# More pairs of k-tiles multiplied with seven block products in a three-product fp32r decoder trunk

## The chip, the cores and the metric

One core of one Trainium2 chip runs the whole program. The metric is the device time of one execution in microseconds (us).

## What is computed

Two decoder layers on 256 tokens of width 2048. Layer 0 mixes tokens by retention (8 heads, keys of 256, values of 512), layer 1 by multi-head latent attention; each mixer is followed by a SwiGLU with an inner width of 5632. The parts that the change touches are three products of the 256 tokens with a weight matrix:

```python
def retention(x, positions, w_in, gn_g, w_out):
    ...
    out = (jax.nn.silu(g.astype(jnp.float32)) * y).astype(x.dtype)
    return out @ w_out

def swiglu(x, w_gu, w_down):
    gate, up = jnp.split(x @ w_gu, [D_FF], axis=-1)
    return (jax.nn.silu(gate) * up) @ w_down
```

## The kernel before

**Splitting.** Every number of a matrix product is split into a high part (a cast to fp32r on ScalarE, here ACT, line 201) and a low part (value minus high part, on VectorE, here DVE, line 202), and a product is made of three matmuls on TensorE, here PE: high by high, high by low, low by high.

**Groups.** `group` multiplies two row tiles of 128 tokens (t = 0, 1) with 1024 columns of a weight matrix, over `kts` k-tiles of 128 rows, into four PSUM banks of 512 columns, b00, b01, b10 and b11 (row tile, column half). A weight tile is 128 x 1024: SyncE's queue (SP) loads it into one of 4 `raw` buffers, ACT writes its high part and DVE its low part, in 5 buffers each (`weights`, tags whi and wlo). An ordinary k-tile takes 12 matmuls of 128 x 512: 2 row tiles, 2 column halves, 3 products. Gate/up runs `group` 11 times per layer (slices j of 512 gate and 512 up columns, 16 k-tiles each), the down projection twice (halves of 1024 columns, 44 k-tiles), the retention output twice (32 k-tiles).

**Pairs by sevens.** Two k-tiles k0 and k1 form a 2 x 2 by 2 x 2 block product: the left side has four 128 x 128 blocks (row tile by k-tile), the right side four 128 x 512 blocks (k-tile by column half). For the pairs in `sevens`, `group` makes it with seven block products in place of eight, 21 matmuls in place of 24. The price is sums. Of the left blocks there are four (`left_sums`, lines 230 to 233, 128 x 128 each, then split into hi and lo, 512 wide); they are made once for gate/up and kept, and once per pair and half in `closing` (`parted`). Of the right blocks there are four too, made anew for each pair: t1 = b00 + b01 and t3 = b01 + b11 in the tile ta, t2 = t1 + b11 and t4 = t2 + b10 in tb (`right_sums`, lines 244 to 247, tsum, 2 buffers). ta and tb are split like weight tiles and take whi and wlo buffers; of tile k0 only the first half is split then, so that a pair by sevens holds four of the five buffers.

**Where the products go.** Products 2, 3 and 4 run straight into banks b00, b01 and b10. Products 1, 5, 6 and 7 have banks of their own (m1, m6 from the six `mm` banks, m5 and m7 the two `misc` banks), which gather over all pairs by sevens of a group. The last pair takes the products in the order 1, 6, 5, 7, 2, 3, 4, the others 1, 2, 3, 5, 7, 6, 4. Behind the last, `combine` (lines 334 to 337) copies m1 to SBUF and forms u and v, and `add` (lines 343 and 345) adds them to the four banks: those of row tile 0 one k-tile after the next (`after + 1`), those of row tile 1 two k-tiles later (`after + 3`).

**Gate/up's end.** After each slice ACT makes fsg (silu of the gate) and DVE fa (times up); fa is transposed on PE some k-tiles later (line 776) and copied by ACT to aT, the left side of the down projection.

**Order.** The program issues in the order of the plan that `group` writes, with small jobs put off by `later`. Each engine works its own queue in order; an instruction that waits holds up what is behind it. Names in the orders below: `gu0_3_w10` is k-tile 10 of slice 3 in layer 0; `_w5_ta` with its `tahi` and `talo` are the sums of pair 5; `mv0`, `mv1`, `mv2` are m1, u and v; `rto` is the retention output, `dn` the down projection.

Of the kernel before, what the change touches and what calls it, by code (L numbers as in the profile page):

```python
# [8 lines left out]
F32 = mybir.dt.float32  # L9
F32R = mybir.dt.float32r  # L10
# [5 lines left out]
P = 128  # L16
# [5 lines left out]
RH, RK, RV = 8, 256, 512  # L22
# [8 lines left out]
G_MIX, G_FFN, G_GN, G_Q, G_KV = 0, 32, 64, 96, 100  # L31
NG = 104

GU_SEVENS = (2, 4)
DN_SEVENS = (2, 6, 10, 14, 18)

C_INV, C_ID, C_MASK, C_TWICE = 0, NF, NF + P, NF + 3 * P
C_DEC = C_TWICE + ROPE
# [16 lines left out]
def trunk(  # L55
# [28 lines left out]
    def misc_bank(name):  # L84
        return ps.tile([P, 512], F32, tag="misc", bufs=2, name=name)
# [30 lines left out]
    def rsqrt(v, n, tag, bufs, name):  # L116
        r = small(n, tag, bufs, name)
        nc.gpsimd.tensor_tensor(out=r, in0=v, in1=mhalf[:, 0:n], op=ALU.pow)
        return r
# [9 lines left out]
    def later(k, fn):  # L129
        order[0] += 1  # L130
        todo.append((steps[0] + k, order[0], fn))
# [63 lines left out]
    wp = ctx.enter_context(tc.tile_pool(name="wp", bufs=1))  # L195
    RAW, WB = 4, 5

    def split(hi, lo, src, g=None):

        if g is None:  # L200
            nc.scalar.copy(out=hi, in_=src)  # L201
            nc.vector.tensor_sub(out=lo, in0=src, in1=hi.bitcast(F32))  # L202
        else:
            nc.scalar.activation(out=hi, in_=src, func=AF.Copy, scale=g)
            nc.vector.scalar_tensor_tensor(
                out=lo, in0=src, scalar=g, in1=hi.bitcast(F32), op0=ALU.mult, op1=ALU.subtract
            )
# [11 lines left out]
    def gain(col, kt):  # L219
        return None if col is None else gcol[:, col + kt : col + kt + 1]  # L220
# [370 lines left out]
    def retention():  # L591
# [32 lines left out]
        def vg_group(h):  # L624
            name = f"rvg{h}"
            return group(h_lhs, DT, tile_load(ret_vg, h, name), name)

        with tc.tile_pool(name="rt_s", bufs=1) as sp:
# [80 lines left out]
            with tc.tile_pool(name="rt_v", bufs=1) as rp:  # L709
                yT = rp.tile([P, RH * 4, NT, P], F32, name="yT")  # L710

                def mixed(h, t, pr, v, sg):
                    y = misc_bank(f"ry{h}{t}")

                    terms = [
                        (pr[a][:, (kb + t) * P : (kb + t + 1) * P], v[b][:, kb, :])
                        for kb in range(t + 1)
                        for a, b in ((0, 0), (0, 1), (1, 0))
                    ]
                    for n, (left, right) in enumerate(terms):  # L720
                        nc.tensor.matmul(y, left, right, start=n == 0, stop=n == len(terms) - 1)  # L721
                    st = rp.tile([P, 6], F32, tag="bst", bufs=4, name="bst")
                    nc.vector.bn_stats(out=st, in_=y)
                    mv = rp.tile([P, 2], F32, tag="bmv", bufs=4, name="bmv")
                    nc.vector.bn_aggr(out=mv, in_=st)
                    ve = rp.tile([P, 1], F32, tag="bve", bufs=4, name="bve")
                    nc.vector.tensor_scalar(ve, mv[:, 1:2], scalar1=EPS, scalar2=None, op0=ALU.add)
                    rs = rsqrt(ve, 1, "grs", 4, "grs")
                    z = rp.tile([P, RV], F32, tag="z", bufs=2, name="z")
                    nc.vector.scalar_tensor_tensor(  # L730
                        out=z, in0=y, scalar=mv[:, 0:1], in1=sg[:, t, :],
                        op0=ALU.subtract, op1=ALU.mult,
                    )
                    nc.vector.tensor_scalar(z, z, scalar1=rs, scalar2=None, op0=ALU.mult)

                    def transposes():
                        tp = misc_bank(f"ztp{h}{t}")
                        for j in range(4):
                            nc.tensor.transpose(
                                tp[:, j * P : (j + 1) * P], z[:, j * P : (j + 1) * P], ident  # L740
                            )
                        for j in range(4):
                            nc.scalar.activation(
                                out=yT[:, h * 4 + j, t, :], in_=tp[:, j * P : (j + 1) * P], func=AF.Copy,
                                scale=gain(G_GN, h * 4 + j),
                            )

                    later(4, transposes)

                for h in range(RH):  # L750
                    if h:
                        banks = vg_group(h)
                    vh = rp.tile([P, NT, RV], F32R, tag="vh", bufs=1, name=f"vh{h}")
                    vl = rp.tile([P, NT, RV], F32R, tag="vl", bufs=1, name=f"vl{h}")
                    ph = rp.tile([P, 3 * P], F32R, tag="ph", bufs=1, name=f"ph{h}")
                    pl = rp.tile([P, 3 * P], F32R, tag="pl", bufs=1, name=f"pl{h}")
                    split(ph, pl, scores[h])
                    sg = rp.tile([P, NT, RV], F32, tag="sg", bufs=1, name=f"sg{h}")
                    for t in range(NT):
                        split(vh[:, t, :], vl[:, t, :], banks[t][0], rx[t])  # L760
                        nc.scalar.activation(
                            out=sg[:, t, :], in_=banks[t][1], func=AF.Silu, scale=rx[t]
                        )
                    for t in range(NT):
                        later(2 + t, lambda h=h, t=t, pr=(ph, pl), v=(vh, vl), sg=sg: mixed(h, t, pr, v, sg))
                closing(lambda k0, n: yT[:, k0 : k0 + n], RH * 4, ret_out, g_mix_post[0], G_FFN, "rto")


    def swiglu(i):
        with tc.tile_pool(name=f"ff{i}", bufs=1) as fp:  # L770
            aT = fp.tile([P, FF // P, NT, P], F32, name=f"aT{i}")

            def transposes(j, t, a):
                tp = misc_bank(f"ftp{i}{j}{t}")
                for b in range(4):
                    nc.tensor.transpose(tp[:, b * P : (b + 1) * P], a[:, b * P : (b + 1) * P], ident)  # L776
                nc.scalar.copy(
                    out=aT[:, j * 4 : j * 4 + 4, t, :], in_=tp.rearrange("p (j q) -> p j q", j=4)
                )


            ins = {}
            held = {}

            def sums():
                return (
                    fp.tile([P, 4, P], F32, tag="sf", bufs=2, name=f"sf{i}"),
                    fp.tile([P, 4, P], F32R, tag="sa", bufs=4, name=f"sh{i}"),
                    fp.tile([P, 4, P], F32R, tag="sa", bufs=4, name=f"sl{i}"),
                )  # L790

            def seen(t, k0, n, part):
                for p in GU_SEVENS:
                    if k0 <= 2 * p < k0 + n:
                        held[t, p] = part[:, 2 * p - k0], part[:, 2 * p - k0 + 1]
                        if (1 - t, p) in held:
                            f, hi, lo = sums()
                            left_sums(*held[0, p], *held[1, p], f, hi, lo)
                            ins[p] = hi, lo

            watch[0] = seen

            for j in range(FF // 512):
                name = f"gu{i}_{j}"
                banks = group(
                    h_lhs, DT, tile_load(w_gu[i], j, name), name, lead=2 if j else 4,
                    sevens=GU_SEVENS if 0 < j else (), left=lambda p: ins[p],
                )
                watch[0] = None
                for t in range(NT):  # L810
                    sg = fp.tile([P, 512], F32, tag="fsg", bufs=2, name="fsg")
                    nc.scalar.activation(out=sg, in_=banks[t][0], func=AF.Silu, scale=rx_next[t])
                    a = fp.tile([P, 512], F32, tag="fa", bufs=2, name="fa")
                    nc.vector.scalar_tensor_tensor(
                        out=a, in0=banks[t][1], scalar=rx_next[t], in1=sg, op0=ALU.mult, op1=ALU.mult
                    )
                    later(2 + t, lambda j=j, t=t, a=a: transposes(j, t, a))
            closing(
                lambda k0, n: aT[:, k0 : k0 + n], FF // P, w_down[i], g_ffn_post[i],
                None if i else G_MIX + DT, f"dn{i}", sevens=DN_SEVENS, sums=sums,  # L820
            )

# [272 lines left out]


    retention()
    swiglu(0)
    mla()
# [92 lines left out]
```

## Time and profile before

| | |
|---|---|
| median of 3 runs | 2454.28 us (2453.28 to 2454.59) |
| the profiled execution | 2454.15 us |
| its span | 2452.3 us, mean granted clock 0.999 |
| PE matmul, weight load | 2438.9 us (99%), 2023.6 us (83%) |
| DVE, ACT | 1799.4 us (73%), 1311.1 us (53%) |

The span runs from the first to the last instruction of the profiled execution. A matmul row lasts longer than its distance to the next one, because matmuls are pipelined; so what one costs is read from stretches of many. PEld is the load of the stationary operand, which runs beside the matmuls.

### The profile page before, as it was taken

What the parts mean: (1) busy time and instruction counts of PE and PEld (TensorE: products, weight loads), DVE (VectorE), ACT (ScalarE), POOL (GpSimd) and SP (SyncE); (2) the same over time, 40 slices, a digit from 0 to 9 for tenths busy, and PEclk for the clock granted to TensorE, in tenths of its full rate; (3) what the DMA queues carried; (4) which work ended last, traced back from release to release, by engine and by line L of the source; (5) the groups of instructions that cost most, each with busy time, mean ns of one, the idle gap of its engine ahead of it and who ended that gap; (6) DMA issues with size and microseconds to landing.
All of it is one profiled execution on the core that took longest, in us unless ns stands there. A gap on an engine that the chain in (4) does not pass through costs nothing.

```text
span 2452.3 us, 30456 instructions
## 1 busy us (share of the span) xinstructions
PE 2438.9 (99%) x11128; PEld 2023.6 (83%) x11128; DVE 1799.4 (73%) x2379; ACT 1311.1 (53%) x1751; POOL 27.1 (1%) x38
## 2 busy tenths in 40 slices
PE   9999999999999999999999999999999999999998
PEld 7888888888888888888888888888888888888887
DVE  7655555555657787787888887876778777788887
ACT  5434544445545554555556666655555554556664
POOL 0000000000000000000000000000000000000000
PEclk9999999999999999999999999999999999999999
DMA  7555555555565566565656655445556656565664
GB/s 261 186 185 178 182 181 181 180 181 181 198 197 189 172 211 200 182 212 180 207 181 210 208 198 162 129 134 193 188 174 210 197 185 211 187 200 183 214 204 155
DMA packets 129607, 463.75 MB, mean 189 GB/s; under 512 B 14640, under 2 KB 15024, under 8 KB 129456
## 3 DMA queue, kind: packets, MB, share of 16 engines
q1 hardware_dynamic: 129456, 461.80, 57.1%
q8 instruction: 87, 1.43, 0.2%
q14 instruction: 64, 0.52, 0.1%
HBM read 459.64 MB, written 2.10 MB: 188 GB/s over the span
## 4 chain that ended last, share of the span: by engine, by line
PE 99%; DMA 0%; DVE 0%; SPq 0%; ACT 0%; issue 0%; DVEq 0%; POOL 0%; POOLq 0%; ACTq 0%
PE gu_b L398 34%; PE dn_b L398 17%; PE rvg_b L398 14%; PE rto_b L398 7%; PE rqk_b L398 7%; PE gu_m L398 4%; PE mlo_b L398 4%; PE q L398 3%; PE dn_m L398 2%; PE mc_b L398 2%; PE ftp L776 1%; PE ry L721 1%; PE htp L434 1%; PE asc L1032 0%; PE rsc L676 0%; PE asc L1029 0%
## 5 line engine op out<-in xcount | busy, mean ns | idle before, releaser
L398 PE MATMUL gu_b<-gu_w_hi,hT 128*128 128x512 f32 x2256 | 640.8, 392 | 0.0
L201 ACT CAST gu_w_hi<-gu_w_raw 128x1024 fp32r<-128x1024 f32 (+1 forms) x352 | 349.4, 1003 | 327.7 <-PE gu_b L398 252.3
L202 DVE TENSOR_TENSOR gu_w_lo<-gu_w_raw,gu_w_hi 128x1024 fp32r<-128x1024 f32 (+1 forms) x352 | 402.7, 1159 | 120.3 <-ACT gu_w_hi L201 120.0
L398 PEld LDWEIGHTS gu_b<-gu_w_hi,hT 128*128 128x128 f32 x2256 | 419.4, 188 | 85.7 <-DVE hT L202 0.9
L398 PE MATMUL gu_b<-gu_w_lo,hT 128*128 128x512 f32 x1128 | 358.2, 390 | 0.0
L398 PE MATMUL rvg_b<-rvg_w_hi,hT 128*128 128x512 f32 x1024 | 280.8, 391 | 0.0
L202 DVE TENSOR_TENSOR rvg_w_lo<-rvg_w_raw,rvg_w_hi 128x1024 fp32r<-128x1024 f32 x128 | 156.4, 1224 | 160.6 <-ACT rvg_w_hi L201 160.6
L398 PEld LDWEIGHTS gu_b<-gu_w_lo,hT 128*128 128x128 f32 x1128 | 211.5, 188 | 44.8 <-DVE gu_w_lo L202 0.6
L201 ACT CAST rvg_w_hi<-rvg_w_raw 128x1024 fp32r<-128x1024 f32 x128 | 134.7, 1053 | 195.8 <-PE rvg_b L398 187.4
L201 ACT CAST dn_w_hi<-dn_w_raw 128x1024 fp32r<-128x1024 f32 (+1 forms) x176 | 174.3, 1003 | 104.1 <-PE dn_b L398 55.9
L398 PEld LDWEIGHTS rvg_b<-rvg_w_hi,hT 128*128 128x128 f32 x1024 | 191.1, 188 | 38.9
L202 DVE TENSOR_TENSOR dn_w_lo<-dn_w_raw,dn_w_hi 128x1024 fp32r<-128x1024 f32 (+1 forms) x176 | 200.0, 1160 | 23.6 <-ACT dn_w_hi L201 22.9
L398 PE MATMUL dn_b<-dn_w_hi,dn_ah 128*128 128x512 f32 x564 | 178.2, 390 | 0.0
L398 PE MATMUL dn_b<-dn_w_lo,dn_ah 128*128 128x512 f32 x564 | 178.0, 390 | 0.0
L398 PE MATMUL dn_b<-dn_w_hi,dn_al 128*128 128x512 f32 x564 | 178.0, 390 | 0.0
L398 PE MATMUL rvg_b<-rvg_w_lo,hT 128*128 128x512 f32 x512 | 158.1, 390 | 0.0
L398 PE MATMUL rqk_b<-rqk_w_hi,hT 128*128 128x512 f32 x512 | 141.0, 393 | 2.0 <-ACT hT L201 1.0
L398 PEld LDWEIGHTS dn_b<-dn_w_lo,dn_ah 128*128 128x128 f32 x564 | 105.9, 188 | 22.0
L398 PEld LDWEIGHTS dn_b<-dn_w_hi,dn_al 128*128 128x128 f32 x564 | 105.9, 188 | 21.9
L398 PEld LDWEIGHTS dn_b<-dn_w_hi,dn_ah 128*128 128x128 f32 x564 | 105.6, 188 | 21.6
L202 DVE TENSOR_TENSOR rqk_w_lo<-rqk_w_raw,rqk_w_hi 128x1024 fp32r<-128x1024 f32 (+1 forms) x65 | 77.5, 1207 | 59.3 <-ACT rqk_w_hi L201 59.3
L201 ACT CAST rqk_w_hi<-rqk_w_raw 128x1024 fp32r<-128x1024 f32 (+1 forms) x65 | 67.4, 1038 | 99.4 <-PE rqk_b L398 90.2
(307 smaller groups left out, 3851.6 us busy)
## 6 DMA issues: line engine op xcount, KB each, us to landing
gu_w_raw<-w_gu SPq DMA_DIRECT2D x352, 512.0 KB, 4.3
dn_w_raw<-w_down SPq DMA_DIRECT2D x176, 512.0 KB, 4.4
rvg_w_raw<-ret_vg SPq DMA_DIRECT2D x128, 512.0 KB, 3.5
rto_w_raw<-ret_out SPq DMA_DIRECT2D x64, 512.0 KB, 3.5
rqk_w_raw<-ret_qk SPq DMA_DIRECT2D x63, 512.0 KB, 4.0
mlo_w_raw<-mla_out SPq DMA_DIRECT2D x32, 512.0 KB, 3.5
uq_w_raw<-mla_up SPq DMA_DIRECT2D x32, 448.0 KB, 3.4
mc_w_raw<-mla_c SPq DMA_DIRECT2D x16, 512.0 KB, 4.6
```

The costliest lines, as they stand in the source:

```text
L201: nc.scalar.copy(out=hi, in_=src)
L202: nc.vector.tensor_sub(out=lo, in0=src, in1=hi.bitcast(F32))
L398: nc.tensor.matmul(out, e[2](), e[3](), start=bank not in begun, stop=ends[bank, bank in added] == n, skip_group_check=bank in added,)
L434: nc.tensor.transpose(tp[:, j * P : (j + 1) * P], xs[:, t, (k0 + j) * P : (k0 + j + 1) * P], ident)
L721: nc.tensor.matmul(y, left, right, start=n == 0, stop=n == len(terms) - 1)
L776: nc.tensor.transpose(tp[:, b * P : (b + 1) * P], a[:, b * P : (b + 1) * P], ident)
```

## The change

The tables at the top of the file choose the pairs. Gate/up takes pairs 2, 3 and 5 of its eight (before: 2 and 4), from slice 1 on; the down projections every third pair, six of 22 (before: every fourth, five); the retention output takes three of 16, for the first time. The third left sums of gate/up live in the buffers of `closing`'s split activations (tags ah and al, 3 each); those of the retention output in buffers of the heads, which are done by then.

```diff
-GU_SEVENS = (2, 4)
-DN_SEVENS = (2, 6, 10, 14, 18)
+GU_SEVENS = (2, 3, 5)
+DN_SEVENS = (2, 5, 8, 11, 14, 17)
+RTO_SEVENS = (2, 6, 10)
...
-                closing(lambda k0, n: yT[:, k0 : k0 + n], RH * 4, ret_out, g_mix_post[0], G_FFN, "rto")
+
+                def sums():
+                    both = ("vh", "vl")[sums.n % 2]
+                    sums.n += 1
+                    s = rp.tile([P, 2, 4, P], F32R, tag=both, bufs=1, name="rs")
+                    f = rp.tile([P, 4, P], F32, tag="sg", bufs=1, name="rsf")
+                    return f, s[:, 0], s[:, 1]
+
+                sums.n = 0
+                closing(
+                    lambda k0, n: yT[:, k0 : k0 + n], RH * 4, ret_out, g_mix_post[0], G_FFN, "rto",
+                    sevens=RTO_SEVENS, sums=sums,
+                )
...
-            def sums():
-                return (
-                    fp.tile([P, 4, P], F32, tag="sf", bufs=2, name=f"sf{i}"),
-                    fp.tile([P, 4, P], F32R, tag="sa", bufs=4, name=f"sh{i}"),
-                    fp.tile([P, 4, P], F32R, tag="sa", bufs=4, name=f"sl{i}"),
-                )
+            def sums(n=0):
+                f = fp.tile([P, 4, P], F32, tag="sf", bufs=2, name=f"sf{i}")
+                if n < 2:
+                    hi = fp.tile([P, 4, P], F32R, tag="sa", bufs=4, name=f"sh{i}")
+                    lo = fp.tile([P, 4, P], F32R, tag="sa", bufs=4, name=f"sl{i}")
+                else:
+                    hi = wp.tile([P, 4, P], F32R, tag="ah", bufs=3, name=f"sh{i}")
+                    lo = wp.tile([P, 4, P], F32R, tag="al", bufs=3, name=f"sl{i}")
+                return f, hi, lo
...
-                            f, hi, lo = sums()
+                            f, hi, lo = sums(len(ins))
```

**DVE, the last pair by sevens of a gate/up slice** (slice 3 of layer 0). Before, from the first low part behind pair 4's sums to tile 10:

```order
L202 TENSOR_TENSOR gu0_3_w6_lo_7172<-gu0_3_w6_raw_7169,gu0_3_w6_hi_7171 128x1024
L202 TENSOR_TENSOR gu0_3_w7_lo_7190<-gu0_3_w7_raw_7187,gu0_3_w7_hi_7189 128x1024
L202 TENSOR_TENSOR gu0_3_w8_lo_7208<-gu0_3_w8_raw_7205,gu0_3_w8_hi_7207 128x512
L202 TENSOR_TENSOR gu0_3_w9_lo_7214<-gu0_3_w9_raw_7211,gu0_3_w9_hi_7213 128x1024
L202 TENSOR_TENSOR gu0_3_w4_talo_7224<-gu0_3_w4_ta_7217,gu0_3_w4_tahi_7223 128x1024
L202 TENSOR_TENSOR gu0_3_w4_tblo_7228<-gu0_3_w4_tb_7218,gu0_3_w4_tbhi_7227 128x1024
L202 TENSOR_TENSOR gu0_3_w10_lo_7262<-gu0_3_w10_raw_7259,gu0_3_w10_hi_7261 128x1024
```

After, from the low part of pair 3's second sum on:

```order
L203 TENSOR_TENSOR gu0_3_w3_tblo_7369<-gu0_3_w3_tb_7359,gu0_3_w3_tbhi_7368 128x1024
L245 TENSOR_TENSOR gu0_3_w5_ta_7441<-gu0_3_w10_raw_7429 128x512
L203 TENSOR_TENSOR gu0_3_w8_lo_7396<-gu0_3_w8_raw_7393,gu0_3_w8_hi_7395 128x1024
L203 TENSOR_TENSOR gu0_3_w9_lo_7414<-gu0_3_w9_raw_7411,gu0_3_w9_hi_7413 128x1024
L203 TENSOR_TENSOR gu0_3_w10_lo_7432<-gu0_3_w10_raw_7429,gu0_3_w10_hi_7431 128x512
L246 TENSOR_TENSOR gu0_3_w5_ta_7441<-gu0_3_w10_raw_7429,gu0_3_w11_raw_7435 128x512
L203 TENSOR_TENSOR gu0_3_w11_lo_7438<-gu0_3_w11_raw_7435,gu0_3_w11_hi_7437 128x1024
L247 TENSOR_TENSOR gu0_3_w5_tb_7442<-gu0_3_w5_ta_7441,gu0_3_w11_raw_7435 128x512
L203 TENSOR_TENSOR gu0_3_w5_talo_7448<-gu0_3_w5_ta_7441,gu0_3_w5_tahi_7447 128x1024
L248 TENSOR_TENSOR gu0_3_w5_tb_7442<-gu0_3_w5_tb_7442,gu0_3_w11_raw_7435 128x512
L203 TENSOR_TENSOR gu0_3_w5_tblo_7452<-gu0_3_w5_tb_7442,gu0_3_w5_tbhi_7451 128x1024
```

Before, the sums of the last pair (four of them, earlier than this piece) were made ahead of the low parts of the two ordinary tiles 6 and 7; now they stand between the low parts of tiles 8 to 11, behind the second sum of the pair two before.

**DVE, the end of the same slice**, from the additions of row tile 0 on. Before:

```order
L345 TENSOR_TENSOR gu0_3_b00_7030<-gu0_3_b00_7030,gu0_3_mv0_7252 128x512
L345 TENSOR_TENSOR gu0_3_b01_7031<-gu0_3_b01_7031,gu0_3_mv1_7253 128x512
L202 TENSOR_TENSOR gu0_3_w14_lo_7339<-gu0_3_w14_raw_7336,gu0_3_w14_hi_7338 128x1024
L345 TENSOR_TENSOR gu0_3_b10_7032<-gu0_3_b10_7032,gu0_3_mv2_7254 128x512
L202 TENSOR_TENSOR gu0_3_w15_lo_7357<-gu0_3_w15_raw_7354,gu0_3_w15_hi_7356 128x1024
L343 TENSOR_TENSOR gu0_3_mv2_7254<-gu0_3_m5_7146,gu0_3_mv2_7254 128x512
L202 TENSOR_TENSOR gu0_4_w0_lo_7387<-gu0_4_w0_raw_7384,gu0_4_w0_hi_7386 128x1024
L345 TENSOR_TENSOR gu0_3_b11_7033<-gu0_3_b11_7033,gu0_3_mv2_7254 128x512
```

After:

```order
L346 TENSOR_TENSOR gu0_3_b00_7207<-gu0_3_b00_7207,gu0_3_mv0_7476 128x512
L346 TENSOR_TENSOR gu0_3_b01_7208<-gu0_3_b01_7208,gu0_3_mv1_7477 128x512
L203 TENSOR_TENSOR gu0_4_w0_lo_7575<-gu0_4_w0_raw_7572,gu0_4_w0_hi_7574 128x1024
L346 TENSOR_TENSOR gu0_3_b10_7209<-gu0_3_b10_7209,gu0_3_mv2_7478 128x512
L203 TENSOR_TENSOR gu0_4_w1_lo_7587<-gu0_4_w1_raw_7584,gu0_4_w1_hi_7586 128x1024
L344 TENSOR_TENSOR gu0_3_mv2_7478<-gu0_3_m5_7323,gu0_3_mv2_7478 128x512
L203 TENSOR_TENSOR gu0_4_w2_lo_7617<-gu0_4_w2_raw_7614,gu0_4_w2_hi_7616 128x1024
L346 TENSOR_TENSOR gu0_3_b11_7210<-gu0_3_b11_7210,gu0_3_mv2_7478 128x512
```

The additions to b10 and b11 stood among the low parts of the slice's last tiles and the next slice's first; now they stand two tiles further on, behind tiles 0, 1 and 2 of the next slice. The additions belong to the slice's last k-tile.

**ACT, the start of the retention output.** Before:

```order
L201 CAST rto0_w4_hi_4646<-rto0_w4_raw_4644 128x1024
L201 CAST rto0_w5_hi_4664<-rto0_w5_raw_4662 128x1024
L201 CAST rto_ah_4640<-yT_2007 128x512
L201 CAST rto0_w6_hi_4686<-rto0_w6_raw_4684 128x1024
L201 CAST rto0_w7_hi_4713<-rto0_w7_raw_4711 128x1024
```

After:

```order
L202 CAST rto0_w4_hi_4654<-rto0_w4_raw_4652 128x512
L202 CAST rto0_w5_hi_4660<-rto0_w5_raw_4658 128x1024
L202 CAST rto_ah_4648<-yT_2007 128x512
L202 CAST rto0_w2_tahi_4670<-rto0_w2_ta_4664 128x1024
L202 CAST rto0_w2_tbhi_4674<-rto0_w2_tb_4665 128x1024
L202 CAST rto_ah_4703<-yT_2007 128x512
L202 CAST rto0_w6_hi_4709<-rto0_w6_raw_4707 128x1024
L202 CAST rto0_w7_hi_4736<-rto0_w7_raw_4734 128x1024
L202 CAST rs_4586<-rsf_4587 128x512
```

The two casts of the sums come in ahead of tile 6, and rs, the split left sums of pair 2 (tiles 4 and 5), stands behind the casts of tiles 6 and 7.

## Rows read from the trace of the kernel before

**Rows 1.** Totals of the page, and busy tenths in 40 slices of the span

```profile
PE 2438.9 (99%) x11128; PEld 2023.6 (83%) x11128; DVE 1799.4 (73%) x2379; ACT 1311.1 (53%) x1751; POOL 27.1 (1%) x38
...
PE   9999999999999999999999999999999999999998
...
DVE  7655555555657787787888887876778777788887
...
PEclk9999999999999999999999999999999999999999
```

**Rows 2.** PE's waits: line, releaser, us in total, times, longest

```profile
PE warm L95 <- DVE mhalf L111: 1.2, 1, 1.2
PE rqk_b L398 <- ACT hT L201: 1.0, 1, 1.0
PE rqk_b L398 <- ACT rqk_w_hi L201: 1.0, 1, 1.0
PE htp L434 <- DMA xs<-x: 0.8, 2, 0.6
PE rqk_b L398 <- DVE rqk_w_lo L202: 0.3, 1, 0.3
PE htp L434 <- DVE xs L497: 0.2, 1, 0.2
```

**Rows 3.** The chain of waits: start us, us, engine, tile, line, instructions

```profile
599.13 149.65 PE rto_b L398 x660
...
1039.57 23.80 PE gu_b L398 x105
...
1246.26 17.00 PE dn_b L398 x75
1267.34 17.00 PE dn_b L398 x75
```

**Rows 4.** The page's costliest groups: one matmul and one weight load of gate/up

```profile
L398 PE MATMUL gu_b<-gu_w_hi,hT 128*128 128x512 f32 x2256 | 640.8, 392 | 0.0
...
L398 PEld LDWEIGHTS gu_b<-gu_w_hi,hT 128*128 128x128 f32 x2256 | 419.4, 188 | 85.7 <-DVE hT L202 0.9
```

**Rows 5.** Timeline of DVE in a gate/up slice: start, us, instruction, idle time before it

```profile
1016.29 0.68 DVE L202 TENSOR_TENSOR gu_w_lo<-gu_w_raw,gu_w_hi 128x512 fp32r<-128x512 f32 x1
1016.89 0.69 DVE L246 TENSOR_TENSOR gu_w_tb<-gu_w_ta,gu_w_raw 128x512 f32<-128x512 f32 x1
1017.61 0.69 DVE L247 TENSOR_TENSOR gu_w_tb<-gu_w_tb,gu_w_raw 128x512 f32<-128x512 f32 x1
1020.02 1.23 DVE L202 TENSOR_TENSOR gu_w_lo<-gu_w_raw,gu_w_hi 128x1024 fp32r<-128x1024 f32 x1 [1.72 <-ACT gu_w_hi L201]
...
1024.78 0.69 DVE L245 TENSOR_TENSOR gu_w_ta<-gu_w_raw 128x512 f32<-128x512 f32 x1 [1.40 <-DMA gu_w_raw<-w_gu]
...
1047.47 1.22 DVE L202 TENSOR_TENSOR gu_w_lo<-gu_w_raw,gu_w_hi 128x1024 fp32r<-128x1024 f32 x1
1048.60 0.69 DVE L343 TENSOR_TENSOR gu_mv<-gu_m,gu_mv 128x512 f32<-128x512 f32 x1
```

**Rows 6.** ACT's groups by form: count, busy us, mean ns, idle before

```profile
L201 ACT CAST gu_w_tahi<-gu_w_ta 128x1024 fp32r<-128x1024 f32 x40 | 42.1, 1054 | 12.5 <-PE gu_b L398 12.2 <-DVE sf L233 0.3
...
L201 ACT CAST sh<-sf 128x512 fp32r<-128x512 f32 x24 | 14.8, 616 | 2.0 <-DVE sf L233 1.7
```

**Rows 7.** Timeline of DVE in the down projection of layer 0

```profile
1303.86 1.23 DVE L202 TENSOR_TENSOR dn_w_tblo<-dn_w_tb,dn_w_tbhi 128x1024 fp32r<-128x1024 f32 x1 [1.47 <-ACT dn_w_tbhi L201]
...
1306.61 4.63 DVE L202 TENSOR_TENSOR dn_w_lo<-dn_w_raw,dn_w_hi 128x1024 fp32r<-128x1024 f32 x4 [0.26 <-ACT dn_w_hi L201]
```

**Rows 8.** One gate/up slice: PE, PEld, DVE, ACT, POOL, clock, DMA share, GB/s

```profile
1003.81:1046.88 43.07, 43.07 (x195) 35.70 (x194) 33.78 (x39) 22.62 (x25) 0.00 (x0) 1.00 0.59 195
```

**Rows 9.** DMA issues of the page: count, size of one, median us to landing

```profile
gu_w_raw<-w_gu SPq DMA_DIRECT2D x352, 512.0 KB, 4.3
```

## Prediction

> **What bounds the kernel now.** I read the totals of the page first. PE is busy 2438.9 us of 2452.3 at full granted clock in every slice, while DVE is busy 73% of the span, ACT 53%; DVE stands at seven or eight tenths in nearly every slice from the 13th on, where gate/up and the down projections lie [rows 1]. A busy PE need not be a PE without waits, so the list of PE's waits comes next: its six rows add up to 4.5 us, all at the start or between layers [rows 2]. The chain of waits agrees: long stretches of matmuls, one after the other. Such a stretch gives the price of a matmul: 23.80 us for 105 in gate/up, 17.00 for 75 in the down projection, 149.65 for 660 in the retention output, 0.2267 us each time [rows 3]. A matmul's own row lasts 0.392 us [rows 4], because its end lies some 0.17 us behind the next one's start; that is no cost, but it is the delay with which a buffer comes free. So every matmul is on the path, and whatever takes matmuls away shortens the kernel, as long as operands come in time.
>
> **What the change takes away.** A pair of k-tiles costs 24 matmuls, a pair by sevens 21. Gate/up has 10 slices per layer with sevens (slice 0 has none): one pair more in each of 20 slices is 60 matmuls. A down projection has 2 halves and two layers, one pair more (six for five) in each of 4 halves: 12. The retention output gets three pairs in each of 2 halves: 18. Together 90, which is also what PE's order shows (10532 rows before, 10442 now, no new ones). 90 x 0.2267 = **20.4 us**: 13.6, 2.7 and 4.1. There are also 30 x 0.68 us fewer of cover for the other engines.
>
> A rule of the Trainium skill speaks for a smaller sum: "TensorE: Matmul & The Clock Gate", section "Back-to-back issue gap", gives about 131 ns per matmul for a stream of weight loads and matmuls of 512 columns; by it the 90 would be worth an estimated 11.8 us. The trace disagrees with 226.7 ns in each of the three stages that the change touches, and the sum goes by the trace.
>
> **What it adds.** For each of the 30 pairs, four sums of 512 columns on DVE (three of 0.60 us start to start and one of 0.72 where it waits for the one before, from 1016.29, 1016.89 and 1017.61), and the low parts of two 1024-wide tiles (1.13 each, as from 1047.47 to 1048.60) [rows 5]; the low part of the pair's first tile shrinks by half (-0.53). That is 3 x 0.60 + 0.72 + 2 x 1.13 - 0.53 = 4.25 us of DVE. ACT gets two casts of 1.05 and saves 0.44 on the halved one (1.05 to 0.62) [rows 6], 1.7 us. Left sums are made per pair in the retention output and the down projections, and once per layer for gate/up: four narrow adds, one 0.62 cast and one low part of 0.60 each [rows 6]. SP's queue keeps its 80 entries; one of them, a load of post-norm gains, stands one place earlier, and nothing waits for it before its half has ended: nothing. The rest costs only where PE waits for it, so I go through the three stages.
>
> *Down projections (4 halves).* Two ordinary pairs lie between sevens now, three before; the cycle of four pairs is 21.08 us (from 1246.26 to 1267.34 [rows 3]). DVE's queue stands idle 1.47 us before the second sum's low part, since the cast before it waits for a buffer that PE holds, and 0.26 us before the run of four low parts that follows [rows 7]. That buffer comes free about 2.7 us before the pair begins; cast (1.05) and low part (1.23) end 0.4 us before the pair's start, and PE asks for them 3.4 us into it, behind 15 matmuls. Slack 3.8 us: nothing lost, 2.7 us gained. DVE's work per three pairs is some 14.3 us of 15.6.
>
> *Retention output (2 halves).* Between sevens lie three ordinary pairs, as in the down projections before, which had no wait: 4.1 us. One exception is the start of half 0. On ACT the cast of pair 2's left sums (rs) stands behind the casts of tiles 6 and 7, and that of tile 7 needs the buffer of tile 4, which PE holds for the first three matmuls of pair 2 (0.68 + 0.17 us). So rs is ready at 0.85 + 1.05 + 0.62 and some handover, 2.6 to 2.9 us into the pair; PE wants it after six matmuls, at 1.36. **About 1.5 us lost, once.** Below, 0, if tile 7's cast does not wait; above 2.5, with the transposes of head 7, which also move behind this pair.
>
> *Gate/up (20 slices).* Here it gets tight. In the slice from 1003.81 to 1046.88 DVE was busy 33.78 of 43.07 us [rows 8]. The new slice has 183 matmuls, 42.4 us, and 38.0 of DVE: 90%, and pairs 2 and 3 stand side by side. I replayed DVE's new order by hand, times counted from PE's start of pair 2 (S). Pair 2 ends at 4.76, pair 3 at 9.52, tiles 8 and 9 at 14.96, pair 5 at 19.72. The second sum of pair 3 needs the buffer of pair 2's first sum, free at 15 x 0.227 + 0.17 = 3.6; with its cast, DVE begins at 4.7. From there DVE has ten pieces of work in its queue without a gap: the low part of that sum, a sum of pair 5, low parts of 8, 9 and half of 10, a sum, low part 11, a sum, the low part of pair 5's first sum, the last sum. 5 x 1.13 + 5 x 0.60 = 8.65, and a row ends 0.09 behind its pitch, so the last sum ends at 13.4. Its cast (1.05) and low part (1.23) end at 15.75. PE asks for them at 14.96 + 4 x 0.227 = 15.87, because the last pair of a slice takes its sixth product second. **Slack 0.12 us.** The second tight place is the slice's end: with the last seven one pair later, the four additions into the banks move behind it, and those of the second half (b10, b11) fall between low parts of the next slice's tiles. By the same prices the addition to b11 ends at 29.66, and PE wants the bank at 29.69. **Slack 0.03 us.**
>
> Both are about as large as what I can't add up: ten prices good to 0.01, and four handovers between engines on the way (buffer to cast, cast to DVE, and both again for pair 5), of which the rows show one kind, the 0.17 of a matmul's end. In the old kernel DVE still had 1.72 us idle in its chain of sums [rows 5], so it had no such place. The bounds per slice: nothing, if both slacks hold; 0.7, if each of the four handovers takes 0.17 more than I gave it. The value nearest to a row is one handover, 0.17, less what is left of the slack of the second place: 0.15 per slice, **3 us**.
>
> **Sum.** 2454.15 (profiled execution, 1.85 outside the span) - 20.4 + 3 + 1.5 = 2438.3; the median of the three runs, 2454.28, is 0.1 above. I forecast **2438 us**, 0.7% less; its own range is 2435 to 2443. What a measurement of this kernel can tell from no change is about 0.2%, 4.9 us.
>
> **The rivals.**
> *All covered.* The slacks hold and the start costs nothing: 2433.7. For it: positive slacks, and a PE that waits delays what follows it too. Against: two places per slice under 0.15 us. Chance 0.20.
> *VectorE takes the gain back in gate/up.* If each slice loses 0.5 to 0.8 us at the two places, the gain of 0.68 is gone: 20 x 0.7 = 14, 2454.15 - 20.4 + 1.5 + 14 = 2449.3, with 2446 to 2452 around it. For it: 90% busy, with ten pieces in a row. Against: 4.3 us of idle time per slice remain. Chance 0.20.
> *A late weight tile makes it slower.* Pair 5's first sum reads tile 10, whose raw buffer (four in all) is that of tile 6 and comes free, by the same replay, at about S + 1.5. In the old trace such a load took 3.5 us: the low part of tile 5 ended at 1020.02 + 1.23, and the sum at 1024.78 had waited for tile 9 until then [rows 5]; the median of all is 4.3 [rows 9]. It lands at S + 5.0 to 5.8, and DVE wants it at 5.8. If it comes x later, the nine pieces from that sum on shift by x, and PE pays x - 0.12 per slice. The gain without it is 20.4 - 1.5 = 18.9, 0.945 per slice, so the sign changes at x = 1.07, and from x = 1.3 (20 x 1.19 = 23.8 = 18.9 + 4.9) the kernel is over 0.2% slower. At x = 1.6 it is 2454.15 - 18.9 + 20 x 1.48 = 2465. For it: the 1.40 us that DVE did wait for a tile at 1024.78. Against: PE waited for none of these loads, and the DMA engines were busy 0.59 of the slice [rows 8], so that a load seldom stands behind many others. Chance 0.06.
> *Only part of the pitch comes back.* If a matmul took from the path only its weight load, a row of 0.188 us [rows 4], the gain would be 90 x 0.188 = 16.9 and the time 2454.15 - 16.9 + 4.5 = 2441.7. Against: matmuls start 0.2267 apart whatever they multiply, and a pair that is gone takes loads and matmuls alike. Chance 0.02. By the Trainium skill, "TensorE: Matmul & The Clock Gate", section "Back-to-back issue gap", it would be an estimated 2446.9 (11.8 in place of 16.9).
> *The change does not do what it says* (pairs that lack their sums would fall back to 24): 2454. The order has the 90 matmuls gone, so 0.02.
>
> **How the numbers follow.** The forecast keeps 0.50. The range from 2433.5 to 2449 takes in the forecast, all covered, and the lower half of VectorE's case, 0.82 together with the smaller pitch. Faster by over 0.2% (under 2449.4): 0.50 + 0.20 + 0.02 + 0.12 of VectorE's case = 0.84. Within: 0.08 of that case and 0.02, 0.10. Slower: 0.06.
>
> **What would show it.** Right: 90 PE matmuls fewer; gate/up slices of 42.4 to 42.6 us; the down projections' cycle of three pairs at 93 - 24 = 69 matmuls, 15.6 us, without a wait; one wait of PE for rs of 1 to 2 us; new waits of PE for the second sum's low part or for b11, each under 0.3 us. Wrong: slices of 43 us and more; a wait of DVE for raw tiles that repeats in every slice just ahead of the sum of pair 5; a granted clock below 1.00; waits in the down projections.

## The result, and the profile after

The changed kernel takes **2440.03 us**, median of four runs (2439.43 to 2441.05), against 2454.41 for the kernel before in the same comparison: 14.4 us less, a ratio of 0.9943 with a 95% interval of 0.9926 to 0.9960. The forecast was 2438, the range 2433.5 to 2449.

The profiled execution took 2439.43 us, its span 2437.6. The page's totals and its row for VectorE, which answer to [rows 1]:

```profile
PE 2425.1 (99%) x11038; PEld 2005.3 (82%) x11038; DVE 1944.2 (80%) x2635; ACT 1367.8 (56%) x1825; POOL 25.0 (1%) x38
...
DVE  7655555557888898898989997876789888899997
...
PEclk9999999999999999999999999999999999999999
```

90 matmuls fewer (11128 to 11038), DVE 145 us busier, at eight or nine tenths in nearly all of gate/up and the down projections, the clock as before. PE is "99% busy" again, as it was. The list of PE's waits is as short as in [rows 2]:

```profile
PE rqk_b L399 <- ACT rqk_w_hi L202: 1.4, 1, 1.4
PE warm L96 <- DVE mhalf L112: 1.2, 1, 1.2
PE rqk_b L399 <- ACT hT L202: 0.7, 1, 0.7
PE rqk_b L399 <- DVE rqk_w_lo L203: 0.4, 1, 0.4
PE gu_m L399 <- DVE gu_w_tblo L203: 0.4, 1, 0.4
```

By this list gate/up lost 0.4 us. The chain of waits tells more, because its pieces have start times (start us, us, engine, tile, line, instructions; answers to [rows 3]). Two stretches of retention output, two neighbouring gate/up slices and two cycles of the down projection (L399 is L398 of the kernel before):

```profile
678.41 17.00 PE rto_b L399 x75
699.49 17.00 PE rto_b L399 x75
...
1039.34 18.36 PE gu_b L399 x81
1082.02 18.37 PE gu_b L399 x81
...
1239.04 11.56 PE dn_b L399 x51
1254.68 11.56 PE dn_b L399 x51
```

Two neighbouring slices of the kernel before, in the same view of its trace:

```profile
996.46 23.80 PE gu_b L398 x105
1039.57 23.80 PE gu_b L398 x105
```

The down projection's cycle is 15.64 us, 69 matmuls at 0.2267 as forecast; the retention output's 21.08, again without a gap. A gate/up slice is 1082.02 - 1039.34 = 42.68 us, where 183 matmuls and the transposes make 42.43 (1039.57 - 996.46 = 43.11 before, less three matmuls). So each slice loses 0.25 us that the wait list doesn't show.

**Where PE lost it.** The timeline of PE in the slice from 1039 backwards, where the last pair by sevens begins, then PEld at the same place, and DVE and ACT ahead of it (start us, us, engine, instruction, idle time before):

```profile
1036.66 0.39 PE L399 MATMUL gu_m<-gu_w_hi,hT 128*128 128x512 f32 x1
1036.89 0.39 PE L399 MATMUL gu_m<-gu_w_tbhi,sh 128*128 128x512 f32 x1
1037.23 0.50 PE L399 MATMUL gu_m<-gu_w_tblo,sh 128*128 128x512 f32 x1
1037.57 0.40 PE L399 MATMUL gu_m<-gu_w_tbhi,sl 128*128 128x512 f32 x1
1037.81 0.39 PE L399 MATMUL gu_m<-gu_w_tahi,sh 128*128 128x512 f32 x1
```

```profile
1036.67 0.19 PEld L399 LDWEIGHTS gu_m<-gu_w_tbhi,sh 128*128 128x128 f32 x1
1037.23 0.19 PEld L399 LDWEIGHTS gu_m<-gu_w_tblo,sh 128*128 128x128 f32 x1 [0.38 <-DVE gu_w_tblo L203]
1037.34 0.19 PEld L399 LDWEIGHTS gu_m<-gu_w_tbhi,sl 128*128 128x128 f32 x1
```

```profile
1025.98 1.23 DVE L203 TENSOR_TENSOR gu_w_tblo<-gu_w_tb,gu_w_tbhi 128x1024 fp32r<-128x1024 f32 x1
...
1034.08 0.68 DVE L248 TENSOR_TENSOR gu_w_tb<-gu_w_tb,gu_w_raw 128x512 f32<-128x512 f32 x1
1035.95 1.22 DVE L203 TENSOR_TENSOR gu_w_tblo<-gu_w_tb,gu_w_tbhi 128x1024 fp32r<-128x1024 f32 x1 [1.19 <-ACT gu_w_tbhi L202]
```

```profile
1024.89 1.06 ACT L202 CAST gu_w_tbhi<-gu_w_tb 128x1024 fp32r<-128x1024 f32 x1 [0.31 <-PE gu_m L399]
...
1034.87 1.05 ACT L202 CAST gu_w_tbhi<-gu_w_tb 128x1024 fp32r<-128x1024 f32 x1 [2.42 <-DVE gu_w_tb L248]
```

Matmuls start 0.227 apart (their pitch) until 1036.89, then come two steps of 0.34, then 0.24 and 0.23 again: 0.23 lost, just where the low part of pair 5's second sum (tblo) is first used. It ended at 1035.95 + 1.22 = 1037.17. The chain that ends there begins with pair 3's second sum, whose cast waited for a buffer that PE held (at 1024.89) and whose low part DVE made at 1025.98. What waited was not the matmul but the weight load ahead of it, which would have begun with the matmul at 1036.89: it sat until 1037.23. That is why the wait list of PE stays silent: matmul rows overlap, so no gap opens between them (the row from 1036.89 lasts until 1037.28). The list of PEld's waits has it, with one count per slice:

```profile
PEld gu_m L399 <- DVE gu_w_tblo L203: 8.0, 20, 0.8
```

20 waits, 0.40 each with the 0.04 that lies between any two loads. By the start times of the matmuls gate/up gained 4.17 us in layer 0 and 3.80 in layer 1 (first matmul of gate/up to first of the down projection, against the same in the old trace), 8.0 of 13.6; the retention output 3.7 of 4.1; the down projections 2.9 of 2.7. The start of the program, which the change doesn't touch, was 0.6 us longer in this execution.

### The profile page after: what moved, and what is told of

Read it like the earlier page. It is cut to its first block, busy times and chain, and to the rows that moved or that the text cites. A ratio compares the mean times of both kernels' runs of the same rounds, so it can differ in the third digit from the quotient of the medians.

```text
span 2437.6 us, 30634 instructions
## 1 busy us (share of the span) xinstructions
PE 2425.1 (99%) x11038; PEld 2005.3 (82%) x11038; DVE 1944.2 (80%) x2635; ACT 1367.8 (56%) x1825; POOL 25.0 (1%) x38
## 4 chain that ended last, share of the span: by engine, by line
PE 98%; DVE 1%; DMA 1%; issue 0%; SPq 0%; ACT 0%; DVEq 0%; POOLq 0%; ACTq 0%
PE gu_b L399 30%; PE dn_b L399 16%; PE rvg_b L399 14%; PE rqk_b L399 7%; PE gu_m L399 6%; PE rto_b L399 6%; PE mlo_b L399 4%; PE q L399 3%; PE dn_m L399 3%; PE mc_b L399 2%; PE ftp L789 1%; PE rto_m L399 1%; PE ry L722 1%; PE htp L435 1%; PE asc L1048 0%; PE rsc L677 0%
## 5 line engine op out<-in xcount | busy, mean ns | idle before, releaser
L399 PE MATMUL gu_b<-gu_w_hi,hT 128*128 128x512 f32 x1976 | 570.5, 392 | 0.0
L202 ACT CAST gu_w_hi<-gu_w_raw 128x1024 fp32r<-128x1024 f32 (+1 forms) x352 | 340.7, 980 | 224.5 <-PE gu_b L399 141.6
L399 PEld LDWEIGHTS gu_b<-gu_w_hi,hT 128*128 128x128 f32 x1976 | 366.7, 188 | 75.2 <-DVE hT L203 0.9
L203 DVE TENSOR_TENSOR gu_w_lo<-gu_w_raw,gu_w_hi 128x1024 fp32r<-128x1024 f32 (+1 forms) x352 | 391.9, 1128 | 33.1 <-ACT gu_w_hi L202 30.9
L399 PE MATMUL gu_b<-gu_w_lo,hT 128*128 128x512 f32 x988 | 316.6, 390 | 0.0
L399 PE MATMUL rvg_b<-rvg_w_hi,hT 128*128 128x512 f32 x1024 | 280.7, 391 | 0.0
L399 PEld LDWEIGHTS rvg_b<-rvg_w_hi,hT 128*128 128x128 f32 x1024 | 191.0, 188 | 38.9
L399 PEld LDWEIGHTS gu_b<-gu_w_lo,hT 128*128 128x128 f32 x988 | 185.2, 188 | 39.4 <-DVE gu_w_lo L203 0.6
L399 PE MATMUL dn_b<-dn_w_hi,dn_al 128*128 128x512 f32 x536 | 170.3, 389 | 0.0
L399 PE MATMUL dn_b<-dn_w_lo,dn_ah 128*128 128x512 f32 x536 | 170.2, 389 | 0.0
L399 PE MATMUL dn_b<-dn_w_hi,dn_ah 128*128 128x512 f32 x536 | 170.0, 390 | 0.0
L399 PE MATMUL rvg_b<-rvg_w_lo,hT 128*128 128x512 f32 x512 | 158.0, 390 | 0.0
L399 PE MATMUL rqk_b<-rqk_w_hi,hT 128*128 128x512 f32 x512 | 141.6, 394 | 2.2 <-ACT rqk_w_hi L202 1.4
L202 ACT CAST rqk_w_hi<-rqk_w_raw 128x1024 fp32r<-128x1024 f32 (+1 forms) x65 | 67.5, 1039 | 100.1 <-PE rqk_b L399 90.6
L399 PEld LDWEIGHTS dn_b<-dn_w_hi,dn_al 128*128 128x128 f32 x536 | 100.6, 188 | 21.0
L399 PEld LDWEIGHTS dn_b<-dn_w_lo,dn_ah 128*128 128x128 f32 x536 | 100.6, 188 | 20.9
L399 PEld LDWEIGHTS dn_b<-dn_w_hi,dn_ah 128*128 128x128 f32 x536 | 100.3, 188 | 20.6
```

What stands on the lines that cost most here:

```text
L399: nc.tensor.matmul(out, e[2](), e[3](), start=bank not in begun, stop=ends[bank, bank in added] == n, skip_group_check=bank in added,)
```

## The experiments

Theory A after the result: gate/up's loss has one place, the last pair's second sum, which is late because the chain of sums starts behind the neighbours 2 and 3, and costs nothing elsewhere. Theory B: VectorE's load is the bound of a slice, wherever PE happens to wait. Theory C: the late additions at the slice's end (b11) are next.

### One order changed: the second sum is asked for later

```diff
-            for i in (1, 6, 5, 7, 2, 3, 4) if final else (1, 2, 3, 5, 7, 6, 4):
+            for i in (1, 5, 6, 7, 2, 3, 4) if final else (1, 2, 3, 5, 7, 6, 4):
```

> The changed kernel, with the last pair by sevens taking its products in the order 1, 5, 6, 7 in place of 1, 6, 5, 7, so that PE asks for the second sum three matmuls (0.68 us) later. Theory A (the 5 us that gate/up lacks come from one place, the low part of pair 5's second sum, which ends 0.34 us behind the weight load that waits for it): that wait goes, slices fall from 42.68 us to 42.4 to 42.5, the time from 2440 to 2434.5 to 2436. Theory B (VectorE at 90% is the bound of a slice, wherever PE happens to wait): the wait moves to another place, slices stay at 42.6 to 42.7, 2439 to 2441. Theory C (the addition to b11 at the slice's end is next): slices of 42.5 to 42.6, 2437 to 2439, with a wait of the second slice half on b11.

Measured: **2433.95 us** (2433.32 to 2435.05), ratio to the kernel before 0.9918 (0.9905 to 0.9931), 6.1 us under the changed kernel. In the chain of waits the slices are 42.43 us; the low part ends at 1034.32 + 1.22 = 1035.54, and the load that wants it begins at 1035.94, 0.40 later, without a wait:

```profile
1037.46 18.36 PE gu_b L399 x81
1079.89 18.36 PE gu_b L399 x81
```

```profile
1034.32 1.22 DVE L203 TENSOR_TENSOR gu_w_tblo<-gu_w_tb,gu_w_tbhi 128x1024 fp32r<-128x1024 f32 x1 [1.20 <-ACT gu_w_tbhi L202]
```

```profile
1035.94 0.19 PEld L399 LDWEIGHTS gu_m<-gu_w_tblo,sh 128*128 128x128 f32 x1
```

One slice by engine (us, PE, PEld, DVE, ACT, POOL, clock, DMA share, GB/s), first of the changed kernel, then of this one:

```profile
1039.34:1082.02 42.68, 42.68 (x193) 35.07 (x192) 38.20 (x46) 24.40 (x27) 0.00 (x0) 1.00 0.60 197
```

```profile
995.03:1037.46 42.43, 42.43 (x193) 35.15 (x192) 38.04 (x45) 24.41 (x27) 0.00 (x0) 1.00 0.61 199
```

The same 38 us of DVE stand in a shorter slice. A holds; B falls, and C too: PE waits for no addition at the slice's end. Gate/up gained 6.8 and 6.6 us in the two layers, which is all of its 13.6 but 0.2. This version is the fastest of all the runs.

### The three parts alone

Gate/up alone, then the down projections alone, then the retention output alone:

```diff
-DN_SEVENS = (2, 5, 8, 11, 14, 17)
-RTO_SEVENS = (2, 6, 10)
+DN_SEVENS = (2, 6, 10, 14, 18)
+RTO_SEVENS = ()
```

> Gate/up's third pair alone; down projections and retention output as before. If the loss lies within gate/up's own slices: 8.0 us gained of 13.6, 2446 to 2447. If it comes from an interplay with the two other parts (shared buffers for the third left sums, for instance): near 13.6, 2441.

```diff
-GU_SEVENS = (2, 3, 5)
-RTO_SEVENS = (2, 6, 10)
+GU_SEVENS = (2, 4)
+RTO_SEVENS = ()
```

> The down projections' sixth pair alone. By the sum of the prediction 12 matmuls, 2.7 us, 2451.7; a loss there (VectorE at 14.3 of 15.6 us) would leave 2452 to 2454.

```diff
-GU_SEVENS = (2, 3, 5)
-DN_SEVENS = (2, 5, 8, 11, 14, 17)
+GU_SEVENS = (2, 4)
+DN_SEVENS = (2, 6, 10, 14, 18)
```

> The retention output's three pairs alone: 18 matmuls, 4.1 us. By the forecast's start (a wait of 1.5 us for rs) 2451.8; by the changed kernel's trace, where PE lost only about 0.4 us in that stage, 2450.7.

Measured beside 2454.51 for the kernel before: gate/up 2446.05 (ratio 0.9967, 0.9954 to 0.9980), down projections 2451.46 (0.9988, 0.9979 to 0.9997), retention output 2450.70 (0.9985, 0.9976 to 0.9994). The gains are 8.5, 3.1 and 3.8 us; their sum, 15.3, is 0.9 over the 14.4 of the whole change, while the single runs scatter by 0.7 to 2.5 us. So no interplay of the parts shows beyond that scatter; the loss is gate/up's own. Of the two figures expected for the retention output, 2450.7 and 2451.8, the time meets the first, though the runs alone (2449.76 to 2452.22) wouldn't settle it; the trace does, below.

### More work on the chain, and the same work off it

VectorE makes one sum twice, for pair 5 in the first kernel, for pair 2 in the second (`_w2` in place of `_w5`):

```diff
-        nc.vector.tensor_add(out=t2, in0=t1, in1=b11)
+        for _ in range(2 if name.startswith("gu") and name.endswith("_w5") else 1):
+            nc.vector.tensor_add(out=t2, in0=t1, in1=b11)
```

> The changed kernel, where VectorE makes one sum of pair 5 twice in every gate/up slice from 1 on (the same values written again, 0.60 us more on the chain that ends in the low part of pair 5's second sum). If that chain is what PE waits for (A): every added 0.60 shows, 20 x 0.60 = 12 us, 2452, slices of 43.3. If PE's loss at that place is a fixed price of something else: 2440 to 2442.

> The same addition of 0.60 us, but to pair 2's sum, where VectorE's timeline shows 0.6 to 0.8 us of idle time behind it. Theory A (one place decides): 2440 to 2441, slices of 42.7. Theory B (VectorE's total of 38 us in 42.4 is the bound): 12 us as in the run with pair 5, 2452.

Measured: off the chain **2440.28** (ratio 0.9942, 0.9929 to 0.9954), slices of 42.68 (four of the 18 distances are up to 0.2 longer), no change in the time, as A said and B did not. On the chain **2445.19** (0.9962, 0.9950 to 0.9975): 5.2 us more, neither the 12 of A nor the 0 to 2 of the rival. The rows tell why. PE's piece of that run, then DVE's:

```profile
1039.13 0.40 PE L400 MATMUL gu_m<-gu_w_tbhi,sh 128*128 128x512 f32 x1
1039.36 0.39 PE L400 MATMUL gu_m<-gu_w_tahi,sh 128*128 128x512 f32 x1
1039.59 0.39 PE L400 MATMUL gu_m<-gu_w_talo,sh 128*128 128x512 f32 x1
1040.18 0.50 PE L400 MATMUL gu_m<-gu_w_tblo,sh 128*128 128x512 f32 x1 [0.20 <-DVE gu_w_tblo L203]
```

```profile
1036.30 0.68 DVE L248 TENSOR_TENSOR gu_w_tb<-gu_w_ta,gu_w_raw 128x512 f32<-128x512 f32 x1
1037.02 0.69 DVE L249 TENSOR_TENSOR gu_w_tb<-gu_w_tb,gu_w_raw 128x512 f32<-128x512 f32 x1
1038.91 1.22 DVE L203 TENSOR_TENSOR gu_w_tblo<-gu_w_tb,gu_w_tbhi 128x1024 fp32r<-128x1024 f32 x1 [1.19 <-ACT gu_w_tbhi L202]
```

The chain did get longer, by 0.73 (the doubled sum stands right ahead of the one that needs it): counted from the start of pair 2 (1023.48) tblo ends at 16.65, in the changed kernel (from 1021.25) at 15.92. But the program's instructions were put in another order with it: two matmuls of product 5 (tahi and talo) now stand ahead of tblo's, 0.45 us of cover. 0.73 - 0.45 = 0.28 per slice, and slices were 42.97 us, 0.29 over 42.68. So the miss was in the cover, and here, where PE already waited, the added lateness came back nearly one for one. The bound of the expectation was wrong because it took PE's order as fixed.

### Without a neighbour for pair 2

```diff
-GU_SEVENS = (2, 3, 5)
+GU_SEVENS = (2, 5)
```

> The changed kernel with gate/up pairs 2 and 5 alone: pair 5 is still the last and the additions still stand at the slice's end, but no pair stands beside pair 2. If the neighbours 2 and 3 make the chain late (the buffer of pair 2's first sum): slices of 43.1 without a wait, 20 x 0.68 = 13.6 us lost and 5.1 won back against the changed kernel, 2448 to 2449. If the late place of the last pair is enough: the wait stays, slices of 43.3 to 43.4, 2453 to 2454.

Measured: 2448.13 (ratio 0.9975, 0.9965 to 0.9985), slices of 43.11, as before, and no wait on tblo of gate/up. So the position of the last pair, with its additions at the end of the slice, costs nothing by itself; the chain is late with pair 3 between and not without it.

### Still more pairs

The order 1, 5, 6, 7, and 6 pairs more: a fourth per half in the retention output, and two of 8 in each half of the latent attention's output projection, whose left sums go into buffers of the heads (`kv0`, `aqkT`).

```diff
-RTO_SEVENS = (2, 6, 10)
+MLO_SEVENS = (2, 5)
+RTO_SEVENS = (2, 5, 8, 11)
...
-                closing(lambda k0, n: oT[:, k0 : k0 + n], AH, mla_out, g_mix_post[1], G_FFN + DT, "mlo")
+                closing(
+                    lambda k0, n: oT[:, k0 : k0 + n], AH, mla_out, g_mix_post[1], G_FFN + DT, "mlo",
+                    sevens=MLO_SEVENS, sums=sums,
+                )
```

> The order 1, 5, 6, 7 for the last pair, a fourth pair per half in the retention output (2, 5, 8, 11), and pairs 2 and 5 of 8 in each half of the latent attention's output projection, whose left sums lie in buffers of the heads. 6 pairs more than with the order alone, 6 x 0.68 = 4.1 us: 2429.9 if all is covered. At the start of the attention output the same kind of wait as forecast for the retention output could take 1 to 2 us: 2431 to 2432.

Measured: 2436.53 (2434.65 to 2437.97; ratio 0.9927, 0.9914 to 0.9939), 2.6 us *more* than with the order alone, and above both figures expected. From its list of PE's waits:

```profile
PE rto_m L400 <- DVE rto_w_tblo L204: 0.9, 1, 0.9
...
PE gu_b L400 <- ACT hT L203: 0.9, 2, 0.6
PE mlo_b L400 <- DVE mlo_b L347: 0.8, 1, 0.8
PE ztp L741 <- DVE rto_mv L338: 0.8, 1, 0.8
PE gu_m L400 <- DVE gu_w_tblo L204: 0.8, 2, 0.4
```

In the stages with added pairs there are now one-off waits of nearly 1 us each. They don't explain all: gate/up gained 5.4 us in each layer there, 2.7 less in all than with the order alone. In layer 1 its slices are 42.43 us throughout, and what is lost (1.3) lies ahead of the first pair by sevens, where PE waits for the left side hT. In layer 0 two slices are 43.0 and 43.2. In the first of these (868.57 to 911.61) VectorE waited for a weight tile just ahead of pair 5's first sum:

```profile
900.07 0.69 DVE L246 TENSOR_TENSOR gu_w_ta<-gu_w_raw 128x512 f32<-128x512 f32 x1 [0.97 <-DMA gu_w_raw<-w_gu]
```

That is the rival with the late tile, and it cost 0.61 us in this slice. The changed kernel has it too, once, in the last slice of layer 1, where tblo's load waited 0.8 in place of 0.4 us:

```profile
2172.14 0.69 DVE L245 TENSOR_TENSOR gu_w_ta<-gu_w_raw 128x512 f32<-128x512 f32 x1 [0.26 <-DMA gu_w_raw<-w_gu]
...
2179.70 1.29 DVE L203 TENSOR_TENSOR sl<-sf,sh 128x512 fp32r<-128x512 f32 x2
```

```profile
2182.58 0.19 PEld L399 LDWEIGHTS gu_m<-gu_w_tblo,sh 128*128 128x128 f32 x1 [0.82 <-DVE gu_w_tblo L203]
```

The tile is only half of it there: tblo ends 0.7 us later than in the slices before, half of it by the tile and half by left sums of the down projection (sl, and two narrow sums not shown), which DVE makes between the last sum and its low part. Why tiles come late in some slices and not in others was not tried, and neither was what makes the stages of the added pairs wait.

## Why the prediction was right, and what in it was off

**The gross sum: right.** 90 matmuls at the pitch of the chain, 20.4 us. With the order of one line changed the kernel is 20.6 us under the one before (2454.51 to 2433.95), so every matmul taken away came back at about 0.227. The rival by the weight load's 0.188 (16.9 us) lies at the edge of that run's interval (16.9 to 23.3 us); what excludes it is the slice, which three matmuls less made 0.68 us shorter (43.11 to 42.43), where 3 x 0.188 would be 0.56. The 131 ns of the Trainium skill's "TensorE: Matmul & The Clock Gate", section "Back-to-back issue gap", an estimated 11.8 us for the 90, do not hold in this case: the trace has 226.7 ns, and 11.8 lies outside that interval.

**Gate/up's stall: right mechanism, under-sized.** The term was 3 us (0.15 per slice); it measured 5.6: 0.20 to 0.26 in the distance of each slice to the next, and 0.4 and 0.65 in the last slices of the two layers, measured against the run with the order changed. Of the two tight places it was the first alone. The prediction had sized its term at the second place (one handover, 0.17, less the slack of 0.03); the same working at the first place (0.17 - 0.12) would have given 0.05 per slice, 1 us. So it is partly luck that the term came out at half of what was measured.

The replay had a slack of 0.12 at the first place, and two of its numbers were off. The chain was 0.17 longer: tblo ended at 15.92 behind S, the start of pair 2 (1021.25), not at 15.75. Its first link began at 4.73 in place of 4.7, the ten pieces of DVE took 8.78 in place of 8.74, and the rest is handovers (the last sum's row ends at 1034.76, the cast begins at 1034.87). And PE asks for an operand when its weight load begins, one pitch (0.227) ahead of the matmul: at 15.64, not 15.87. Put right, the slack is 15.64 - 15.92 = -0.28, and with the handover to PEld the load was 0.34 late (1037.23 less 1036.89). Of that PE lost 0.23 to 0.25; 0.11 came back at the next load, which began 0.11 behind the late one (1037.34) in place of 0.227.

The second place held, but not by its 0.03. The replay had the addition to b11 end at 29.66 behind S. It ended at 29.55 in the changed kernel and, counted from 1019.62, at 29.30 in the run with the order changed, where PE lost nothing ahead of it:

```profile
1050.10 0.70 DVE L346 TENSOR_TENSOR gu_b<-gu_b,gu_mv 128x512 f32<-128x512 f32 x1
```

```profile
1048.22 0.69 DVE L346 TENSOR_TENSOR gu_b<-gu_b,gu_mv 128x512 f32<-128x512 f32 x1
```

By the replay's own numbers (29.66, and a load one pitch ahead of 29.69) PE would have waited here as well.

**The start of the retention output: the time was right, the wait was not.** The prediction had rs ready 2.6 to 2.9 us into pair 2. It was: the pair began at 587.77, rs was there at 590.55, and a load took it at 590.61. But ACT had not waited for tile 4's buffer, as the prediction had it; it had waited for PE ahead of the activations' cast (rto_ah), and from there on it worked without a wait, through the casts of two weight tiles to rs. That the time agreed is luck in part.

```profile
587.51 0.62 ACT L202 CAST rto_ah<-yT 128x512 fp32r<-128x512 f32 x1 [2.53 <-PE rto_b L399]
588.04 2.00 ACT L202 CAST rto_w_hi<-rto_w_raw 128x1024 fp32r<-128x1024 f32 x2
589.94 0.61 ACT L202 CAST rs<-rsf 128x512 fp32r<-128x512 f32 x1
```

```profile
589.58 0.64 PEld L399 LDWEIGHTS rto_b<-rto_w_hi,rto_ah 128*128 128x128 f32 x3
590.61 0.19 PEld L399 LDWEIGHTS rto_b<-rto_w_hi,rs 128*128 128x128 f32 x1 [0.38 <-ACT rs L202]
```

And PE did not ask after six matmuls. Its order at this place is not that of the program's text: product 4, which needs no left sum, and three matmuls of an ordinary tile (the three loads from 589.58) stand ahead of rs. So PE asked after twelve, and lost 0.23 in place of 1.5. The step that failed is "PE wants it after six matmuls, at 1.36": it came from the code, where PE's order, available with the change, would have told it. The stage as a whole lost 0.4.

**Down projections: right.** No wait, 2.9 us by the trace, 3.1 in the run alone.

**The sum.** The sum was made for the profiled execution: 2438.3, and 2439.43 was measured. Gate/up cost 2.6 us more than put, the retention output 1.1 less, which leaves 1.5; the start of that execution was 0.6 longer, and the stages outside the change and the tail of the span were 1 us shorter. So the forecast's distance of 2 us is small also because a cost put too low and one put too high offset each other.

**The rivals.** "VectorE takes the gain back" had the right engine and not enough of it: 0.25 of the 0.5 to 0.8 us per slice, and not through its load (the doubled sum off the chain was free). "A late weight tile" ahead of pair 5's first sum occurs, but in one slice of 20. "All covered" is what one change of order makes of it.

## What to carry to other kernels

Two numbers decide what moving a bottleneck's partner costs: when the last operand is ready, and when the waiting engine asks. Take the second from the engine's own instruction order, not from the program text, and for a matmul take the start of its weight load. Where a slack comes out at a tenth of a microsecond per repetition, look for an order that asks later before counting on it: here swapping two of seven products was worth 6 us, as much as two fifths of the whole change. And a loss of 0.25 us per slice may be in no list of waits; the distance between the starts of like pieces shows it.

## What the runs showed of the hardware that was not expected

- Where a late matmul costs its time can't be told from the matmuls' rows alone. By their starts (1036.89, 1037.23, 1037.57) the 0.23 falls in two halves, on the late one and on the next; by their ends (1037.28, 1037.73, 1037.97), which the profile models, all of it falls on the late one. The sum is the same.
- A weight load that was 0.34 us late cost PE 0.23 to 0.25; in the retention output one that was 0.35 late (590.61, one pitch ahead of the matmul due at 590.49) cost 0.23.
- PE's busy share stood at 99% and its own list of waits at 0.4 us for gate/up while it lost 5.6 us there. The Trainium skill, "Perfetto Trace Analysis", section "Identifying the Most-Contended Engine", says that the matmul busy share is not a good measure of how close a kernel is to the engine's limit, because pipelined matmuls look smaller in a trace, and names the weight loads' busy share beside another measure instead. The trace agrees on the first, since the matmuls' 99% stayed where it was; the loads' share hardly moved either (83% to 82%), and it was the waits in their rows that held the loss.
